# A decoder layer on one core: the bias and the sums of weight tiles in another order on the DMA queues

## The chip, the core and the metric

The kernel runs on one core of one Trainium2 chip. A core has five engines with instruction streams of their own: TensorE (PE in the profile) for matrix products, VectorE (DVE) and ScalarE (ACT) for elementwise work, GpSimd (POOL) and SyncE (SP). The streams wait for each other by semaphores. DMAs are issued by an engine's stream, each of which is worked off in order, and all of them share the core's 16 DMA engines. The metric is the time of one execution on the device in microseconds (us); lower is better.

## The reference

One layer: RMS norm, a pooling mixer with a residual, RMS norm, a gated feed-forward net with a short convolution, and a residual. x is 1024 rows (sequence) by 1024 columns (model), all in float32; the hidden width is 2816.

```python
def pool_mixer(x, w, b, scale):            # windows 2, 4, 8, 16, one for each quarter of the columns
    ...
        groups.append(window_sum / count - xf[..., gi * POOL_GROUP:(gi + 1) * POOL_GROUP])
    d = jnp.stack(groups, axis=2)
    y = jnp.einsum('bsgc,gcd->bsgd', d, w.astype(jnp.float32)).reshape(bsz, seq, D_MODEL) + b
    return (scale * y).astype(x.dtype)

def conv_ffn(x, w_in, conv_w, conv_b, w_out):
    h = causal_depthwise_conv(x @ w_in, conv_w, conv_b)
    val, gate = jnp.split(h, 2, axis=-1)
    return (jax.nn.silu(gate) * val) @ w_out

def reference(x, ...):
    h = rms_norm(x, norm_mix_g[layer])
    x = x + pool_mixer(h, pool_w[j], pool_b[j], pool_scale[j])
    f = conv_ffn(rms_norm(x, norm_ffn_g[layer]), ffn_w_in[layer], ...)
    return x + f
```

## The kernel before

**Stages.** First the mixer, for eight blocks of 128 rows (x0 to x7). For each block j: statistics of x (`stat`, tiles `st_a`), a band matrix scaled by them (`mixer_norm`, `bandr`), the window sums as products of x with that band (`mixer_window`, PSUM tile `psd`; x is the stationary operand, line 212), the mixer's weights (`mixer_out`, `psy`, line 296), the addition of `psy` to x on VectorE (line 304, in place; the result x1 is stored to `x1_dram`, line 305), statistics again (`st_b`), the second normalization (`ffn_norm`, `n2`, line 316), and a transposition on TensorE (`ffn_operand`, `pst`, line 331). The stages of neighbouring blocks overlap.

Then the first product of the feed-forward net, in a Strassen-like form. x1's normalized transpose and each weight tile are cut in quarters, and seven products (P1 to P7, `STEPS`) of sums of quarters replace eight. The operands made from x1 are B11, B21, T1, B22, T2, T3 and T4. Those of weight tile n (22 tiles; `win`, with quarters a11, a12, a21, a22) are A11, A12, A22 and four sums: S3 = a11 + a21, S1 = a21 + a22 (written into a21), S2 = a11 + S1 (into a11), S4 = a12 + S2 (into a12). So S1 may be made only after S3 has read a21, S2 after S1 and after A11 was split, and S4 after S2 and after A12 was split. Each float32 operand is split into a high part (ScalarE, line 95) and a rest (VectorE, line 96), and a product is three matmuls for each of four steps (line 416). The second product of the net (line 779) follows the same pattern, from memory.

**The bias and the sums by DMA.** For blocks 0 to 3 the mixer's bias is two matmuls more (line 301). For blocks 4 to 7 (`BY_DMA`) GpSimd's queue adds it to x: `bias_into` issues a DMA that accumulates `bias_b`, the bias spread over 128 partitions, into x (line 244). It must come after `psd` of that block has read x, and before line 304. `bias_b` itself is loaded from a row in device memory (line 240). The sums S3, S1, S2 and S4 of tiles 0 and 1 are accumulating DMAs of the same queue (line 373; `sums_in` by its argument `step`), and so are S3 and S1 of all later tiles, whose S2 and S4 VectorE makes. S3 begins as a second load of a11 into a small tile of its own (line 379, SyncE's queue). An accumulating DMA of line 373 moves 256 KB, one of line 244 moves 512 KB.

**What sets the order.** A scheduler places each instruction in its engine's stream from the order in which the code issues it; `tc.issue_after(m)` puts what follows behind instruction m in that order, which is an order of streams and adds no semaphore. The loop at line 531 runs over j and issues for each j: the norm of block j, the window of block j - 1 with its bias, the output of block j - 2 and its norm, the transposition of block j - 4, and then at chosen j the loads and sums of weight tiles 0 and 1 (lines 550 to 561) and their first splits (`prep_event(k)`, where k counts in `events`: 0 and 1 are A11 of tiles 0 and 1, 2 and 3 are A12, 4 and 5 are S1, 6 and 7 are S4, 8 is S2 of tile 0). Line 541 issues event 4; lines 572 to 575 issue events 5 to 8. A stream waits at an instruction until its semaphores have come, and all that is behind it in that stream waits too.

Of the kernel before, what the change touches and what calls it, by code (L numbers as in the profile page):

```python
# [14 lines left out]
P = 128  # L15
S = 1024
D = 1024
F = 2816
NS = S // P
# [30 lines left out]
NH = 512  # L50
# [17 lines left out]
def trunk_kernel(ctx: ExitStack, tc: tile.TileContext, x, consts, par, rows, pool_w, w_in, w_out, out):  # L68
    nc = tc.nc
# [98 lines left out]
    marks = {}  # L168
# [66 lines left out]
    bias_row = dram.tile([1, D], F32, tag="bias_row", name="bias_row")  # L235
    biased = {}

    def bias_spread():
        biased["tile"] = work.tile([P, D], F32, tag="ha", name="bias_b", bufs=1)
        nc.gpsimd.dma_start(biased["tile"], bias_row.to_broadcast([P, D]))  # L240

    def bias_into(j):
        if j >= BY_DMA:
# [2 lines left out]
    def pool_bias():  # L246
        marks["bias"] = nc.scalar.activation(bias8[:, 0, :], b8, AF.Copy).ins
        marks["bias_dve"] = nc.vector.tensor_tensor(bias8[:, 1, :], b8, bias8[:, 0, :].bitcast(F32), ALU.subtract).ins
        nc.gpsimd.dma_start(bias_row.rearrange("o (k p) -> (o k) p", p=P), b8)
        for l in range(2):  # L250
            m = nc.sync.dma_start(bias_hl[l : l + 1, :].bitcast(F32), bias8[:, l, :].bitcast(F32)).ins
        with tc.issue_after(m):
            for j in range(3, NS):
                load_x(j)
            marks["loads"] = nc.sync.dma_start(par_sb[:, :GM], par[:, :GM]).ins

    def gain_rows():
# [33 lines left out]
    def mixer_out(j, stats=True):  # L291
        dh = ds.pop(j)
        ps = bank2(f"psy{j}")
        for c in range(NK):
            o = ps[:, c // 2 * GRP : (c // 2 + 1) * GRP]
            m = nc.tensor.matmul(  # L296
                o, dh[:, c, :P], wps[:, c, :], start=c % 4 == 0, stop=j >= BY_DMA and c % 4 == 3, skip_group_check=True
            )
        for h in range(0 if j >= BY_DMA else 2):
            cols = slice(h * NH, (h + 1) * NH)  # L300
            m = nc.tensor.matmul(ps[:, cols], ones, bias_hl[:, cols], start=False, stop=True, skip_group_check=True)
        marks[f"psy{j}"] = m.ins
        x1 = n2s[j] = xs.pop(j)
        marks[j] = nc.vector.tensor_tensor(x1, ps, x1, ALU.add).ins  # L304
        nc.sync.dma_start(x1_dram[j * P : (j + 1) * P, :], x1)
        if stats:
            mixer_out_stats(j)

# [58 lines left out]
    def tmp(name):  # L367
        return work.tile([P, NH], F32, tag="sum", name=name, bufs=3)

    def sums_in(n, step):  # L370

        def more(out, a):
            nc.gpsimd.dma_start(out, a, accum_op=ALU.add)  # L373

        a11, a12, a21, a22 = (raws[n][:, i, k * NH : (k + 1) * NH] for i in range(2) for k in range(2))
        if step == 0:
            s3 = sums[n, "S3"] = tmp(f"S3_{n}")
            with tc.issue_after(marks["loads"]):
                nc.sync.dma_start(s3, w_in[order[n]][:, 0, :NH])
            more(s3, a21)  # L380
        if step == 0 and n > 1 or step == 2:
            more(a21, a22)
        if step == 1:
            sums[n, "S2"] = a11
            more(a11, a21)
            sums[n, "S4"] = a12
            more(a12, a11)

    def prep_in(n, op):
        a11, a12, a21, a22 = (raws[n][:, i, k * NH : (k + 1) * NH] for i in range(2) for k in range(2))  # L390
        if op in ("S1", "S2") and (n, "S3") not in sums:
            s3 = sums[n, "S3"] = tmp(f"S3_{n}")
            add(s3, a11, a21)
            add(a21, a21, a22)
        if op in ("S2", "S4") and (n, "S2") not in sums:
            sums[n, "S2"] = a11
            add(a11, a21, a11)
        if op == "S4" and (n, "S4") not in sums:
            add(a12, a12, a11)
        if op == "S3":  # L400
            src = sums[n, "S3"]
        else:
            src = {"A11": a11, "A12": a12, "S1": a21, "A22": a22, "S2": a11, "S4": a12}[op]
        log = []
        aops[n, op] = split(src, f"{op}s_{n}", log)
        marks[op, n] = log[0]
        if op == "A22" and n + 2 < NF:
            load_in(n + 2)
            sums_in(n + 2, 0)

    def product(bank, a, b, opens):
        m = 0
# [104 lines left out]
        mixer_weights(scale_b, range(1, 2 * NG))  # L517
    with tc.issue_after(marks["psd0"]), tc.issue_after(marks["bias"]):
        gains.append(gain_rows())
    with tc.issue_after(marks["gain_load"]):  # L520
        bias_spread()
    with tc.issue_after(marks["gain"]), tc.issue_after(marks["wps"]):
        stat(2)
    with tc.issue_after(marks["gain_pe"]), tc.issue_after(marks["a2"]), tc.issue_after(marks["wps"]):
# [6 lines left out]
    for j in range(2, NS + 4):  # L531
# [17 lines left out]
            ffn_operand(j - 4)  # L549
        if j in (4, 6):  # L550
            load_in(j // 2 - 2)
            sums_in(j // 2 - 2, 0)
        if j in (5, 6):
            with tc.issue_after(biased[j - 1]):
                sums_in(j - 5, 2)
        if 6 <= j <= 8:
            with tc.issue_after(marks[j - 2]), tc.issue_after(marks[f"b{j - 3}"]):
                for k in {6: (0,), 7: (1, 2), 8: (3,)}[j]:
                    prep_event(k)
        if j in (7, 8):  # L560
            sums_in(j - 7, 1)
        if j in (8, 10, 11):
            event((8, 10, 11).index(j))
        stat(j + 1)
# [6 lines left out]
        nops[b] = nop_tile(nop_b, b)  # L571
    for k in range(4, 4 + LOOK):
        if k != 4:
            with tc.issue_after(marks["T1"][1] if k == 8 else marks[NS - 1]):
                prep_event(k)
    s0, s1 = slice(0, NH), slice(NH, S)
    lo, hi = slice(0, 4), slice(4, 8)
# [284 lines left out]
```

## Time and profile before

| | us |
|---|---|
| median of 3 runs (range) | 671.14 (670.97 to 672.75) |
| the profiled execution | 671.28 |
| its span, first to last instruction | 669.6 |
| TensorE busy | 660.2 (99%) |
| VectorE busy | 567.9 (85%) |
| ScalarE busy | 336.6 (50%) |
| GpSimd busy | 53.6 (8%) |
| mean granted TensorE clock | 0.997 |

Busy time of TensorE is modelled and its matmuls overlap, so a busy TensorE isn't one at its peak; waits and the mean spacing of matmuls say more. In a row of the timeline stand the start, the duration, the engine, the line, the instruction, what it writes and reads, and in brackets the idle time before it and what ended that. Buffer numbers are left out of names: `x` may be any of the eight blocks, which then follows from the order. SPq is SyncE's DMA queue. For an issued DMA the duration is that of the issue; its landing comes later and is given by another view, or by the chain of waits, where a row that begins with DMA lasts from issue to landing.

### The profile page before, as it was taken

The numbers are of one execution on the slowest core, as the hardware profiler recorded it, in microseconds if no ns is written. First come the engines' busy times: TensorE is split into PE (matmuls) and PEld (weight loads), VectorE is DVE, ScalarE is ACT, GpSimd is POOL, SyncE is SP. The second block draws the span as 40 slices with busy tenths as digits, with TensorE's granted clock in tenths as the row PEclk, the third lists the DMA queues.
The fourth block names the chain that finished last, engine by engine and source line by source line (L and its number), as shares of the span: only waits on it lengthen the run. The fifth ranks groups of instructions, "written<-read, shape, count | busy, mean of one in ns | idle before, by whom it ended". The sixth has DMA issues, their size and how long they took to land.

```text
span 669.6 us, 8664 instructions
## 1 busy us (share of the span) xinstructions
PE 660.2 (99%) x3126; PEld 575.1 (86%) x3126; DVE 567.9 (85%) x845; ACT 336.6 (50%) x521; POOL 53.6 (8%) x81
## 2 busy tenths in 40 slices
PE   8998999999999999999999999999999999999997
PEld 6897878888888888888888888888888888888886
DVE  5778999998888888888888888887987988999995
ACT  5786655555445544444544444554554444444441
POOL 5022020110011111111001101100000000000000
PEclk9998999999999999999999999999999999999999
DMA  7999263544544454444444444429999810122231
GB/s 233 360 244 209 85 151 125 159 145 122 142 120 111 132 141 142 143 130 125 138 142 127 111 140 125 114 94 332 342 341 342 290 47 1 62 96 80 63 126 63
DMA packets 42386, 103.73 MB, mean 155 GB/s; under 512 B 4796, under 2 KB 6760, under 8 KB 39528
## 3 DMA queue, kind: packets, MB, share of 16 engines
q1 hardware_dynamic: 34464, 87.43, 37.1%
q0 software_dynamic: 7872, 15.75, 13.4%
q8 instruction: 24, 0.39, 0.3%
q14 instruction: 18, 0.15, 0.1%
q10 hardware_dynamic: 8, 0.00, 0.0%
HBM read 68.55 MB, written 19.93 MB: 132 GB/s over the span
## 4 chain that ended last, share of the span: by engine, by line
PE 90%; DMA 4%; DVE 3%; ACT 1%; issue 1%; SPq 0%; POOL 0%; ACTq 0%; POOLq 0%; DVEq 0%
PE oP L779 29%; PE Y L416 25%; PE X L416 17%; PE Z L416 15%; PE psy L296 2%; DMA S<-win 1%; DMA S<-in_w_in_dram 1%; DMA x<-bias_b 1%; DMA cst<-in_consts_dram 1%; DVE T L351 1%; PE pst L331 1%; PE psd L212 0%; DVE x L304 0%; DVE n2f L588 0%; ACT B L350 0%
## 5 line engine op out<-in xcount | busy, mean ns | idle before, releaser
L779 PE MATMUL oP<-oBP,oAP 128*128 128x512 f32 (+1 forms) x924 | 198.9, 378 | 0.1
L779 PEld LDWEIGHTS oP<-oBP,oAP 128*128 128x128 f32 x924 | 174.0, 189 | 25.0 <-DVE oBP L96 0.5
L416 PE MATMUL X<-B,A11s 128*128 128x512 f32 x264 | 61.5, 380 | 0.0
L416 PE MATMUL Y<-T,S3s 128*128 128x512 f32 x264 | 60.8, 380 | 0.4 <-DVE q L445 0.4
L416 PE MATMUL Y<-T,A22s 128*128 128x512 f32 x264 | 60.9, 380 | 0.0
L416 PE MATMUL Z<-T,S1s 128*128 128x512 f32 x264 | 60.8, 379 | 0.0
L416 PE MATMUL X<-B,A12s 128*128 128x512 f32 x264 | 60.7, 379 | 0.0
L416 PE MATMUL Y<-T,S2s 128*128 128x512 f32 x264 | 60.6, 379 | 0.0
L416 PE MATMUL Z<-B,S4s 128*128 128x512 f32 x264 | 60.5, 379 | 0.0
L416 PEld LDWEIGHTS Y<-T,S3s 128*128 128x128 f32 x264 | 49.7, 189 | 8.2 <-DVE q L445 1.2
L416 PEld LDWEIGHTS Y<-T,A22s 128*128 128x128 f32 x264 | 49.7, 189 | 7.9 <-DVE hb L453 0.6
L416 PEld LDWEIGHTS Z<-T,S1s 128*128 128x128 f32 x264 | 49.8, 189 | 7.5 <-DVE T L351 0.4
L416 PEld LDWEIGHTS Z<-B,S4s 128*128 128x128 f32 x264 | 49.8, 189 | 7.3 <-DVE r L450 0.3
L416 PEld LDWEIGHTS Y<-T,S2s 128*128 128x128 f32 x264 | 49.9, 189 | 7.1
L416 PEld LDWEIGHTS X<-B,A11s 128*128 128x128 f32 x264 | 49.7, 189 | 7.3 <-DVE A11s L96 0.4
L416 PEld LDWEIGHTS X<-B,A12s 128*128 128x128 f32 x264 | 49.8, 189 | 7.0
L95 ACT ACTIVATE oBP<-blk 128x512 fp32r<-128x512 f32 x53 | 33.1, 625 | 44.2 <-PE oP L779 30.6
L474 ACT ACTIVATE gate<-gate 128x1024 f32<-128x1024 f32 x22 | 23.2, 1056 | 49.3 <-DVE gate L465 49.3
L95 ACT ACTIVATE oAP<-blk 128x512 fp32r<-128x512 f32 x55 | 34.1, 620 | 19.6 <-DVE blk L362 17.0
L96 DVE TENSOR_TENSOR oBP<-blk,oBP 128x512 fp32r<-128x512 f32 x53 | 36.5, 688 | 8.6 <-ACT oBP L95 6.6
L96 DVE TENSOR_TENSOR oAP<-blk,oAP 128x512 fp32r<-128x512 f32 x55 | 37.7, 685 | 2.9 <-ACT oAP L95 2.9
L373 POOL DMA_DIRECT2D S<-win x22 | 19.2, 873 | 254.0 <-DMA win<-in_w_in_dram 253.4
(157 smaller groups left out, 965.9 us busy)
## 6 DMA issues: line engine op xcount, KB each, us to landing
win<-in_w_in_dram SPq DMA_DIRECT2D x22, 1024.0 KB, 4.9
g_dram<-val SPq DMA_DIRECT2D x22, 512.0 KB, 2.6
blk<-g_dram SPq DMA_DIRECT2D x33, 256.0 KB, 5.3
blk<-in_w_out_dram SPq DMA_DIRECT2D x31, 256.0 KB, 5.2
win<-win POOLq DMA_DIRECT2D x26, 256.0 KB, 3.7
S<-in_w_in_dram SPq DMA_DIRECT2D x22, 256.0 KB, 3.3
S<-win POOLq DMA_DIRECT2D x22, 256.0 KB, 4.2
A12s<-g_dram SPq DMA_DIRECT2D x22, 256.0 KB, 5.2
```

Of the source, the lines that this page charges most:

```text
L95: nc.scalar.activation(t[:, 0, :], src, AF.Copy)
L96: m = nc.vector.tensor_tensor(t[:, 1, :], src, t[:, 0, :].bitcast(F32), ALU.subtract)
L296: m = nc.tensor.matmul(o, dh[:, c, :P], wps[:, c, :], start=c % 4 == 0, stop=j >= BY_DMA and c % 4 == 3, skip_group_check=True)
L331: nc.tensor.transpose(ps[:, c * P : (c + 1) * P], n2[:, c * P : (c + 1) * P], ident)
L351: return hi, nc.vector.tensor_tensor(l, src, h.bitcast(F32), ALU.subtract).ins
L373: nc.gpsimd.dma_start(out, a, accum_op=ALU.add)
L416: nc.tensor.matmul(bank, a[:, i, ks], woven(b[:, l, k, :]), start=opens and m == 0, stop=m == 11, skip_group_check=not opens)
L474: nc.scalar.activation(gate, gate, AF.Silu)
L779: nc.tensor.matmul(bank, a[:, u, i * P : (i + 1) * P], woven(b[:, v, :])[:, c.start // 2 : c.stop // 2, :], start=opens and first, stop=g ...
```

## The change

`bias_b` is loaded by SyncE's queue, between the loads of x4 and x5. `sums_in` takes the names of the parts that it is to issue, and the loop issues them in another order among the bias additions: S3 of tile 0, bias of block 5, S3 of tile 1 and S1 of tile 0, bias of block 6, S2 of tile 0, bias of block 7, then the rest. The second load of a11 (for S3) of tile 2 and of later ones is issued after the store of x1's last block instead of after the first loads. Events 5 to 8 are issued after the second statistics of block 7 as well. The same DMAs are issued as before, with the same bytes, and the engines do the same arithmetic.

```diff
     def bias_spread():
         biased["tile"] = work.tile([P, D], F32, tag="ha", name="bias_b", bufs=1)
-        nc.gpsimd.dma_start(biased["tile"], bias_row.to_broadcast([P, D]))
+        nc.sync.dma_start(biased["tile"], bias_row.to_broadcast([P, D]))
...
             for j in range(3, NS):
                 load_x(j)
+                if j == 4:
+                    bias_spread()
...
-        nc.sync.dma_start(x1_dram[j * P : (j + 1) * P, :], x1)
+        marks[f"x1_{j}"] = nc.sync.dma_start(x1_dram[j * P : (j + 1) * P, :], x1).ins
...
-    def sums_in(n, step):
+    def sums_in(n, *names):
...
-        if step == 0:
-            s3 = sums[n, "S3"] = tmp(f"S3_{n}")
-            with tc.issue_after(marks["loads"]):
-                nc.sync.dma_start(s3, w_in[order[n]][:, 0, :NH])
-            more(s3, a21)
-        if step == 0 and n > 1 or step == 2:
-            more(a21, a22)
-        if step == 1:
-            sums[n, "S2"] = a11
-            more(a11, a21)
-            sums[n, "S4"] = a12
-            more(a12, a11)
+        for name in names:
+            if name == "load":
+                s3 = sums[n, "S3"] = tmp(f"S3_{n}")
+                with tc.issue_after(marks["loads" if n < 2 else f"x1_{NS - 1}"]):
+                    nc.sync.dma_start(s3, w_in[order[n]][:, 0, :NH])
+            elif name == "S3":
+                more(sums[n, "S3"], a21)
+            elif name == "S1":
+                more(a21, a22)
+            elif name == "S2":
+                sums[n, "S2"] = a11
+                more(a11, a21)
+            else:
+                sums[n, "S4"] = a12
+                more(a12, a11)
...
             load_in(n + 2)
-            sums_in(n + 2, 0)
+            sums_in(n + 2, "load", "S3", "S1")
...
-    with tc.issue_after(marks["gain_load"]):
-        bias_spread()
...
             load_in(j // 2 - 2)
-            sums_in(j // 2 - 2, 0)
-        if j in (5, 6):
-            with tc.issue_after(biased[j - 1]):
-                sums_in(j - 5, 2)
+            sums_in(j // 2 - 2, "load")
+        if j == 4:
+            sums_in(0, "S3")
+        if j == 6:
+            with tc.issue_after(biased[5]):
+                sums_in(1, "S3")
+                sums_in(0, "S1")
...
-        if j in (7, 8):
-            sums_in(j - 7, 1)
+        if j == 7:
+            with tc.issue_after(biased[6]):
+                sums_in(0, "S2")
+        if j == 8:
+            with tc.issue_after(biased[7]):
+                sums_in(1, "S1")
+                sums_in(0, "S4")
+                sums_in(1, "S2", "S4")
...
         if k != 4:
-            with tc.issue_after(marks["T1"][1] if k == 8 else marks[NS - 1]):
+            with tc.issue_after(marks["T1"][1] if k == 8 else marks[NS - 1]), tc.issue_after(marks[f"b{NS - 1}"]):
                 prep_event(k)
```

The streams of the two kernels differ in three places that matter here. First GpSimd's queue from the bias of block 4 on, before the change (a row `win0<-win0` is S1, S2 or S4 of tile 0, in that order; the numbers at the ends of names are buffers):

```order
L244 DMA x4_227<-bias_b_250 128x1024
L373 DMA S3_0_416<-win0_414 128x512
L373 DMA win0_414<-win0_414 128x512
L373 DMA S3_1_544<-win1_542 128x512
L244 DMA x5_229<-bias_b_250 128x1024
L373 DMA win1_542<-win1_542 128x512
L373 DMA win0_414<-win0_414 128x512
L244 DMA x6_231<-bias_b_250 128x1024
L373 DMA win1_542<-win1_542 128x512
L244 DMA x7_233<-bias_b_250 128x1024
L373 DMA win0_414<-win0_414 128x512
L373 DMA win1_542<-win1_542 128x512
```

and with it:

```order
L244 DMA x4_227<-bias_b_229 128x1024
L375 DMA S3_0_416<-win0_414 128x512
L244 DMA x5_231<-bias_b_229 128x1024
L375 DMA S3_1_543<-win1_541 128x512
L375 DMA win0_414<-win0_414 128x512
L244 DMA x6_233<-bias_b_229 128x1024
L375 DMA win0_414<-win0_414 128x512
L244 DMA x7_235<-bias_b_229 128x1024
L375 DMA win1_541<-win1_541 128x512
L375 DMA win0_414<-win0_414 128x512
L375 DMA win1_541<-win1_541 128x512 x2
```

The bias of block 5 has moved ahead of S1 of tile 0 and of S3 of tile 1, and that of block 7 ahead of S1 of tile 1; all three sums of tile 1 (S1, S2, S4) now stand behind the last bias.

Second, SyncE's queue from the load of x4 on, before:

```order
L110 DMA x4_227<-in_x_dram 128x1024
L110 DMA x5_229<-in_x_dram 128x1024
L110 DMA x6_231<-in_x_dram 128x1024
L110 DMA x7_233<-in_x_dram 128x1024
L255 DMA par_sb_124<-in_par_dram 128x176
L305 DMA x1_dram_150<-x0_134 128x1024
L305 DMA x1_dram_150<-x1_138 128x1024
L359 DMA win0_414<-in_w_in_dram 128x2048
L379 DMA S3_0_416<-in_w_in_dram 128x512
L359 DMA win1_542<-in_w_in_dram 128x2048
L305 DMA x1_dram_150<-x2_144 128x1024
L379 DMA S3_1_544<-in_w_in_dram 128x512
```

and with the change:

```order
L110 DMA x4_227<-in_x_dram 128x1024
L240 DMA bias_b_229<-bias_row_149 128x1024
L110 DMA x5_231<-in_x_dram 128x1024
L110 DMA x6_233<-in_x_dram 128x1024
L110 DMA x7_235<-in_x_dram 128x1024
L257 DMA par_sb_124<-in_par_dram 128x176
L307 DMA x1_dram_150<-x0_134 128x1024
L307 DMA x1_dram_150<-x1_138 128x1024
L361 DMA win0_414<-in_w_in_dram 128x2048
L307 DMA x1_dram_150<-x2_144 128x1024
L382 DMA S3_0_416<-in_w_in_dram 128x512
L361 DMA win1_541<-in_w_in_dram 128x2048
```

The load of `bias_b` is new in this queue. The store of x1's block 2 now stands ahead of the S3 load of tile 0 and of tile 1's load; the S3 load of tile 2, which stood right behind the last row shown of before, now comes after the store of block 7.

Third, ScalarE around the end of the mixer, before (`S1s_1` is the split of S1 of tile 1, `st_b7` the second statistics of block 7, `q1` and `ha` are copies of products out of PSUM):

```order
L95 ACTIVATE S1s_0_683<-win0_414 128x512
L95 ACTIVATE S1s_1_793<-win1_542 128x512
L343 ACTIVATE n2f_151<-pst4_649 128x4x2x64
L180 ACTIVATE junk_b6_639,st_b6_640<-x6_231 128x1024
L350 ACTIVATE T1_153<-n2f_151 128x8x64
L181 ACTIVATE st_b6_640<-st_b6_640,eps_t_87 128x1
L439 ACTIVATE q1_0_681<-X0_668 128x512
L95 ACTIVATE S4s_0_796<-win0_414 128x512
L343 ACTIVATE n2f_151<-pst5_707 128x4x2x64
L180 ACTIVATE junk_b7_697,st_b7_698<-x7_233 128x1024
L343 ACTIVATE n2f_151<-pst6_721 128x4x2x64
L181 ACTIVATE st_b7_698<-st_b7_698,eps_t_87 128x1
```

and with the change:

```order
L345 ACTIVATE n2f_151<-pst5_707 128x4x2x64
L180 ACTIVATE junk_b7_697,st_b7_698<-x7_235 128x1024
L352 ACTIVATE T1_153<-n2f_151 128x8x64
L181 ACTIVATE st_b7_698<-st_b7_698,eps_t_87 128x1
L345 ACTIVATE n2f_151<-pst6_721 128x4x2x64
L95 ACTIVATE S1s_1_793<-win1_541 128x512
L95 ACTIVATE S4s_0_796<-win0_414 128x512
L352 ACTIVATE T1_153<-n2f_151 128x8x64
L444 ACTIVATE q1_1_748<-X1_735 128x512
L95 ACTIVATE S4s_1_799<-win1_541 128x512
L95 ACTIVATE S2s_0_802<-win0_414 128x512
L447 ACTIVATE ha0_776<-X0_668 128x512
```

The split of S1 of tile 1 and that of S4 of tile 0 have moved behind `st_b7`, and one half of the T1 operand now stands ahead of them.

## The prediction, made before the changed kernel ran

> **What bounds the kernel now.** I read the page first, for the span and the granted TensorE clock in 40 slices.
>
> ```profile
> span 669.6 us, 8664 instructions
> ...
> PEclk9998999999999999999999999999999999999999
> ```
>
> TensorE is the bound nearly everywhere, at full clock: only the fourth slice (50 to 67 us) falls to 8 tenths. So what can be won lies where TensorE waits or is slow, and for that I read the waits of the first 130 us.
>
> ```profile
> DVE x L304 <- DMA x<-bias_b: 5.8, 2, 4.2
> ...
> PE psy L296 <- DVE x L304: 2.3, 1, 2.3
> ```
>
> VectorE's addition of the mixer's output to x (line 304) waits 5.8 us, in two pieces, for GpSimd's DMA that adds the bias to x; behind the longer piece (4.2) TensorE waits 2.3 us. The chain of waits (start, us, what) shows what comes before and after.
>
> ```profile
> 33.37 8.63 DMA S<-win
> ...
> 43.59 7.64 DMA x<-bias_b
> ...
> 52.60 5.41 PE psy L296 x16
> ...
> 61.47 3.45 PE psy L296 x16
> ```
>
> The bias DMA at 43.59 lands at 51.23, just before the addition. The 16 matmuls of the next `psy` then take 5.41 us, the same 16 later 3.45. The stretches of 1 us give the reason (last three numbers: granted clock, DMA share, GB/s):
>
> ```profile
> 53.00:54.00 1.00, 1.00 (x4) 0.83 (x3) 1.00 (x3) 0.95 (x3) 0.56 (x2) 0.50 1.17 205
> ...
> 56.00:57.00 1.00, 1.00 (x6) 0.83 (x5) 0.95 (x1) 1.00 (x3) 0.07 (x1) 0.81 1.00 279
> ```
>
> The clock is at half from 53 to about 56.4 us. So the place costs TensorE 2.29 us of waiting (the row at 52.60 less the end of the matmuls at 49.69, 50.30) and 5.41 - 3.45 = 1.96 us of slow matmuls: **4.25 us**. No other place of this trace shows such a loss.
>
> **Why the bias is late.** TensorE had released the x tile (block 5) much earlier:
>
> ```profile
> 37.33 0.65 PE L212 MATMUL psd5x<-bandr,x 128*128 128x144 f32 x4
> ...
> 43.54 0.65 PE L212 MATMUL psd6x<-bandr,x 128*128 128x144 f32 x4
> ...
> 44.03 3.62 PE L296 MATMUL psy<-wps,dh 128*128 128x256 f32 x16
> ...
> 49.69 0.61 PE L212 MATMUL psd7x<-bandr,x 128*128 128x128 f32 x4
> ```
>
> The bias for block 5 may go once `psd5` has read x, at 37.98. It went at 43.59. GpSimd's queue (start, us of the issue) shows what stood ahead of it:
>
> ```profile
> 42.51 0.85 POOL L373 DMA_DIRECT2D win<-win  x1 [8.27 <-DVE bandr L189]
> ...
> 43.05 1.19 POOL L373 DMA_DIRECT2D S<-win  x1
> ...
> 43.59 1.53 POOL L244 DMA_DIRECT2D x<-bias_b  x1
> ...
> 49.92 1.55 POOL L244 DMA_DIRECT2D x<-bias_b  x1
> ...
> 53.97 1.21 POOL L244 DMA_DIRECT2D x<-bias_b  x1
> ...
> 60.66 0.86 POOL L373 DMA_DIRECT2D win<-win  x1 [4.59 <-DVE A12s L96]
> ```
>
> The three x rows are blocks 5, 6 and 7. Ahead of block 5 stand S1 of weight tile 0 at 42.51, which could go only when S3 of that tile (33.37 + 8.63 = 42.00) had landed, and S3 of tile 1. VectorE, meanwhile:
>
> ```profile
> 45.83 1.28 DVE L316 SCALAR_TENSOR_TENSOR n<-x,st_b,gain_b 128x1024 f32<-128x1024 f32 x1
> ...
> 51.32 1.23 DVE L304 TENSOR_TENSOR x<-psy,x 128x1024 f32<-128x1024 f32 x1 [4.21 <-DMA x<-bias_b]
> ...
> 58.54 1.23 DVE L304 TENSOR_TENSOR x<-psy,x 128x1024 f32<-128x1024 f32 x1 [1.59 <-DMA x<-bias_b]
> ```
>
> It is idle from 47.11 to 51.32 (4.21) and again 1.59 us for block 6. `psy` of block 5 is done at 44.03 + 3.62 = 47.65, so block 5's addition could have run 3.7 us earlier.
>
> **The change, part by part.**
>
> *Order in GpSimd's queue.* No DMA is added; block 5 goes ahead of S3 and S1. It now has only S3 of tile 0 before it. That waits for its load on SyncE's queue, where the change puts the store of x1 block 2 first:
>
> ```profile
> 24.01 0.47 SPq L359 DMA_DIRECT2D win<-in_w_in_dram  x1
> ...
> 24.53 0.67 SPq L379 DMA_DIRECT2D S<-in_w_in_dram  x1
> ...
> 25.39 0.53 SPq L359 DMA_DIRECT2D win<-in_w_in_dram  x1
> ...
> 29.84 0.33 SPq L305 DMA_DIRECT2D x_dram<-x  x1
> ...
> 30.21 1.25 SPq L379 DMA_DIRECT2D S<-in_w_in_dram  x2
> ```
>
> The load is issued after 29.84 instead of at 24.53, about 5.7 us later, and the second weight tile (25.39) as much. From issue to its use at 33.37 the load took at most 8.84 us before; with the same it would be usable at 39.05, at worst. At best it has only 0.79 MB (the store and itself) to move. Rates come from the DMA view of 30 to 66 us:
>
> ```profile
> q0 software_dynamic: 1721, 4.19, 64.2%
> ...
> q1 hardware_dynamic: 1276, 4.43, 33.7%
> ...
> win<-win POOLq DMA_DIRECT2D x6, 256.0 KB, 5.4
> ```
>
> In these 36 us the accumulating queue took 36 x 0.642 / 4.19 = 5.5 us per MB and SyncE's 36 x 0.337 / 4.43 = 2.7. An accumulate of 256 KB costs the engines 1.45 us, one of 512 KB 2.9; a plain 512 KB costs 1.44, and the weight tile 2.9. The engines are full here (97.9% together), so I make the landings a running sum from 29.84. Until block 5's bias is done there are: store 1.44, S3 load 0.72, tile 1 2.87, its S3 load 0.72, block 4's bias 2.89, S3 of tile 0 1.45, a store 1.44, block 5 2.89, in all 14.4, so 44.3. It is wanted at 47.65. With the whole 7.64 us of its row from 38.5, it lands at 46.2. Even held until 39.05 plus the 0.88 us or so of an issue, it comes at 47.6. So **block 5's wait goes: -2.29 us**, and as TensorE then has no gap, the half clock goes too: **-1.96 us**.
>
> *What is late next.* Without the gap `psy` of block 6 follows `psd7` at 50.30 and ends near 53.7. Block 6's bias may go at 44.19 (after `psd6`); the sum goes on by S3 and S1 (1.45 each), a store and itself to 51.5. So 1.59 us of VectorE waiting goes too, but TensorE is then the later one, and I count nothing for it (if all of it counted, 4.21 + 1.59 = 5.80 would be the most that the change can bring). Block 7's bias goes after 50.30 and the sum gives 57.3; it is wanted at 61.31 + 3.45 - 4.25 = 60.5.
>
> *The parts of tile 1.* They are moved behind block 7, one after the other, as each reads what the last wrote: S1, S2, S4. In the sum S1 is in at 58.7. S2 and S4 follow: at least 2 x 1.45 more (61.6), at most twice the median row of 5.4 and 0.54 for an issue (43.05 to 43.59), which gives 70.6. I take 67.7, two thirds of the way up: the engines are less full by then, but the 5.4 holds more than packets. The last reader is ScalarE's split of S4:
>
> ```profile
> 46.98 0.65 ACT L95 ACTIVATE A11s<-win 128x512 fp32r<-128x512 f32 x1
> ...
> 69.80 0.62 ACT L95 ACTIVATE S4s<-win 128x512 fp32r<-128x512 f32 x1
> ...
> 71.98 0.63 ACT L95 ACTIVATE S2s<-win 128x512 fp32r<-128x512 f32 x1 [1.56 <-DVE n L316]
> ...
> 73.20 0.60 ACT L343 ACTIVATE n2f<-pst 128x512 f32<-128x512 f32 x1
> ```
>
> From that split at 69.80 to the copy of the last transposed block at 73.20 lie 3.40 us, 1.56 of them idle, so 1.84 of work stands in ScalarE's queue behind S4. The copy would start 4.25 earlier, at 68.95; S4 must be there by 67.1. At 67.7 it is 0.6 late. **+0.6 us** (0 to 3.5). What waits for that copy is VectorE's T1, and TensorE's products of it:
>
> ```profile
> 72.09 1.06 PE L331 MATMUL pst<-cst,n 128*128 128x128 f32 x8
> ...
> 75.37 5.60 PE L416 MATMUL Z<-T,S1s 128*128 128x512 f32 x24
> ```
>
> *Three splits later.* Line 574's new condition puts three splits of weight parts behind the statistics of block 7. S1 of tile 1 is used only after 12 matmuls of the row at 75.37, and VectorE gets one T1 subtraction less ahead of the last normalization in exchange. Cost 0; were the cover gone, a split is 0.62 us.
>
> *The bias's spread.* It moves from GpSimd's queue to SyncE's, ahead of the loads of blocks 5 to 7, with the same 512 KB.
>
> ```profile
> L110 SPq DMA_DIRECT2D x<-in_x_dram x1: 430/430/430, 13.7 to 13.7; - x1
> ...
> DMA to landing us min/median/max: 7.6/7.6/7.6
> ...
> 25.03 1.04 ACT L180 ACTIVATE junk_a<-x 128x1024 bf16<-128x1024 f32 x1
> ```
>
> Block 5's load landed at 21.3 and is read first at 25.03. One more transfer ahead costs it 1.44 us by the rate above: 22.7. It costs 0 while those 3.7 us cover it; without cover, 1.4.
>
> *The S3 load of tile 2* (the second of the two issues at 30.21) goes behind the last store. It frees 0.7 us of full engines; it is added to only when tile 2 has come, after the products of tile 0. Cost 0. Tile 1 comes some 6 us later; its first split ran at 46.98, when the sum above has it in by 36, so 0.
>
> **Sum.** -2.29 - 1.96 + 0.6 = -3.65. The profiled execution took 671.28 us (span 669.6 and 1.7 around it), 0.14 over the median of the runs: 667.6, or **667.5 us** beside the median of 671.14.
>
> **The rivals.**
>
> *B, the slow clock has another cause.* [...] If the half clock came from something else, it would come again, and the change would bring 3.65 - 1.96 = 1.7: 669.5.
>
> *C, the wait moves to block 6.* Its bias stands behind S1 of tile 0, which waits for S3's accumulate. If the S3 load needs its 8.84 again (39.05) and the accumulate its 8.63 (47.7), block 6 goes at 48.2 and lands 7.64 later, at 55.9, 2.2 after `psy`. VectorE is that much late; it had about 1 us of reserve before TensorE needs the last normalization, so 1.2 of the gain go: 668.8. Against it: the engines' sum has both in 4 us earlier.
>
> *D, slower: the serial parts of tile 1.* S1, S2 and S4 of tile 1 now all lie behind block 7. With block 7 landing at 50.9 + 7.64 = 58.5, S1 at 60.0, one of the other two as slow as the 8.63 row, one at 5.4, and two issues, S4 is in at 75.1. ScalarE then stands still with the last copies behind it, and the start of T1's products is 75.1 - 67.1 = 8.0 late against 4.25 won: +3.75, 674.9. It decides from a landing of 71.4 on (67.1 + 4.25). For it: before, only S2 and S4 came behind block 6. Against it: the bytes hardly change, and the sum has S1 in at 58.7, with only the last two stores beside S2 and S4.
>
> **Chances.** Forecast 0.62, B 0.11, C 0.14, D 0.13. Within 0.3% (2.0 us, about what runs of this kernel can tell from no change) lie B, a third of C and little of the forecast; so faster 0.70, same 0.17, slower 0.13. The range begins at 671.14 - 5.80, 665.4, and reaches to the forecast with its S4 term at 3.5 (670.4), over B and C: 665.4 to 670.6. It leaves out D.
>
> **What would show it.** Right: line 304 no longer waits for the bias, `psy` of block 6 starts near 50.3 and takes 3.45, the granted clock is 1.00 in every slice after the start, and the products of T1 start near 71.7. The order is shown wrong if block 5's bias is issued later than 40, the S4 term if ScalarE waits over 1 us for S4 of tile 1. A half clock without a wait before it would prove B; a wait of line 304 for block 6, C; an S4 landing after 71.4, D. A difference that arises after 130 us would be none of these.

## The result, and the profile after

The changed kernel takes **667.88 us** (667.48 to 669.01, 6 runs) against 671.16 of the kernel before (670.97 to 672.75, 6 runs of the same comparison): a ratio of 0.9949, 95% interval 0.9936 to 0.9962. The prediction was 667.5 in a range of 665.4 to 670.6, with 0.70 on faster. The profiled execution took 667.48 us. Of all executions compared below one, of number 3, ran in a slower state (692.11 us at a mean granted clock of 0.949), and it isn't counted. First the page of the changed kernel, which answers to the two lines shown of before:

```profile
span 665.8 us, 8664 instructions
...
PEclk9999999999999999999999999999999999999999
```

The fourth slice of the clock, 8 tenths before, is 9 or more, like all others. The waits of the first 130 us (what waited, for what: us in total, times, longest):

```profile
ACT S4s L95 <- DMA win<-win: 1.8, 1, 1.8
...
DVE x L306 <- DMA x<-bias_b: 1.0, 1, 1.0
```

Line 306 (304 before) waited 5.8 us for the bias; 1.0 is left. ScalarE's wait for S4 of tile 1 is new at this place. VectorE's additions of blocks 5, 6 and 7:

```profile
47.45 1.23 DVE L306 TENSOR_TENSOR x<-psy,x 128x1024 f32<-128x1024 f32 x1 [0.25 <-PE psy L298]
...
54.13 1.23 DVE L306 TENSOR_TENSOR x<-psy,x 128x1024 f32<-128x1024 f32 x1 [1.04 <-DMA x<-bias_b]
...
60.42 1.23 DVE L306 TENSOR_TENSOR x<-psy,x 128x1024 f32<-128x1024 f32 x1
```

Block 5 waits for nothing but the matmuls. Block 6 has the 1.04. GpSimd's queue shows why (S3 of tile 0, bias 5, S1 of tile 0, bias 6, bias 7, S4 of tile 1):

```profile
36.99 0.87 POOL L375 DMA_DIRECT2D S<-win  x1 [4.49 <-DMA S<-in_w_in_dram]
...
38.23 0.85 POOL L244 DMA_DIRECT2D x<-bias_b  x1 [0.37 <-ACT st_b L181]
...
45.15 0.85 POOL L375 DMA_DIRECT2D win<-win  x1 [1.37 <-DVE psd6x L284]
...
45.69 1.19 POOL L244 DMA_DIRECT2D x<-bias_b  x1
...
52.07 1.20 POOL L244 DMA_DIRECT2D x<-bias_b  x1
...
64.55 0.86 POOL L375 DMA_DIRECT2D win<-win  x1 [3.60 <-DVE st_b L184]
```

Block 5's bias goes at 38.23, not 43.59, about half a microsecond after `psd5` has read x (37.68). The view of that one DMA gives its landing:

```profile
L244 POOL DMA_DIRECT2D x<-bias_b x1: 851/851/851, 38.2 to 38.2; - x1
...
DMA to landing us min/median/max: 9.1/9.1/9.1
```

38.23 + 9.1 = 47.3, when the addition was wanted at 47.45. So it was in time by about 0.1 us, and not by the 3 that the prediction's running sum gave (44.3). Block 6's had to follow S1 of tile 0 at 45.15, which waited for S3's accumulate, issued at 36.99 and in 7.6 later, at 44.6. On TensorE:

```profile
49.40 0.61 PE L212 MATMUL psd7x<-bandr,x 128*128 128x128 f32 x4
...
49.84 3.62 PE L298 MATMUL psy<-wps,dh 128*128 128x256 f32 x16
...
53.30 1.04 PE L333 MATMUL pst<-cst,n 128*128 128x128 f32 x8
...
67.58 1.06 PE L333 MATMUL pst<-cst,n 128*128 128x128 f32 x8 [0.26 <-DVE n L318]
...
71.54 0.46 PE L421 MATMUL Z<-T,S1s 128*128 128x512 f32 x1 [0.31 <-ACT T L352]
...
72.24 5.23 PE L421 MATMUL Z<-T,S1s 128*128 128x512 f32 x23 [0.24 <-DVE T L353]
...
86.73 2.86 PE L421 MATMUL Y<-T,S3s 128*128 128x512 f32 x12 [0.41 <-DVE q L450]
```

`psy` of block 6 follows `psd7` without a wait and its 16 matmuls are over by 53.30 or so, where the next row begins, 3.46 after their start. The products of T1 start at 71.54 instead of 75.37, but with two short pauses (0.31 and 0.24). ScalarE has their cause, the split of S4 of tile 1 with the copy behind it:

```profile
67.96 0.64 ACT L95 ACTIVATE S4s<-win 128x512 fp32r<-128x512 f32 x1 [1.79 <-DMA win<-win]
...
69.49 0.59 ACT L345 ACTIVATE n2f<-pst 128x512 f32<-128x512 f32 x1
```

The start of an execution shifts by some tenths of a microsecond from run to run, here by 49.69 - 49.40 = 0.29. I therefore measure from the row of `psd7x` to the first product with S3 of tile 0, which the kernel before had at

```profile
90.44 2.86 PE L416 MATMUL Y<-T,S3s 128*128 128x512 f32 x12 [0.41 <-DVE q L445]
```

that is 90.44 - 49.69 = 40.75 before and 86.73 - 49.40 = 37.33 after: **3.42 us** gained between these two points. A second profile of each kernel gives 40.78 (number 8) and 37.30 (number 11).

### The profile page after: what moved, and what is told of

Read it like the earlier page. It is cut to its first block, busy times and chain, and to the rows that moved or that the text cites. A ratio compares the mean times of both kernels' runs of the same rounds, so it can differ in the third digit from the quotient of the medians.

```text
span 665.8 us, 8664 instructions
## 1 busy us (share of the span) xinstructions
PE 658.3 (99%) x3126; PEld 573.9 (86%) x3126; DVE 567.8 (85%) x845; ACT 336.6 (51%) x521; POOL 53.0 (8%) x80
## 4 chain that ended last, share of the span: by engine, by line
PE 95%; DVE 2%; ACT 1%; issue 1%; DMA 1%; POOL 0%; ACTq 0%; POOLq 0%
PE oP L791 29%; PE Y L421 25%; PE X L421 16%; PE Z L421 16%; PE psy L298 4%; PE psd L212 2%; PE pst L333 1%; DVE T L353 1%; DMA win<-win 1%; PE idle_ps L152 0%; DVE n2f L600 0%; PE ps_scale L224 0%; ACT B L352 0%; PE psy L303 0%; DVE oBP L96 0%
## 5 line engine op out<-in xcount | busy, mean ns | idle before, releaser
L469 DVE SCALAR_TENSOR_TENSOR val<-ha,par_sb,val 128x1023 f32<-128x1023 f32 x22 | 28.2, 1282 | 13.2 <-ACT val L468 13.2
```

Source lines behind the costliest of these rows:

```text
L469: nc.vector.scalar_tensor_tensor(t[:, 1:], src[:, : S - 1], w[1], t[:, 1:], op0=ALU.mult, op1=ALU.add)
```

## The experiments

The theory: the gain is the wait for block 5's bias and what followed from it, and the order of GpSimd's queue brings it; the spread, the load and the splits bring nothing by themselves. Rivals: one of the other edits carries it; the half clock is a separate loss, or none at all; what is left (the S4 wait, block 6's wait) is or is not on the path to the end.

### 1. The order undone, everything else kept

```diff
-        if j == 4:
-            sums_in(0, "S3")
-        if j == 6: ... sums_in(1, "S3"); sums_in(0, "S1")
...
+            sums_in(j // 2 - 2, "load", "S3")
+        if j in (5, 6):
+            with tc.issue_after(biased[j - 1]):
+                sums_in(j - 5, "S1")
...
-        if j == 7: ... sums_in(0, "S2")
-        if j == 8: ... sums_in(1, "S1"); sums_in(0, "S4"); sums_in(1, "S2", "S4")
+        if j in (7, 8):
+            sums_in(j - 7, "S2", "S4")
```

> The changed kernel with GpSimd's queue in the order of before; the bias's spread on SyncE's queue, the later splits and the later load stay. My theory (the order carries the gain): S3 of tile 0 still gets its load only near 36.9, its accumulate lands near 45, so S1 goes at 45 and block 5's bias at about 46, landing near 53.5; line 306 waits about 6 us for it, TensorE 4.5, the clock goes to half for some 3.4 us, and the time is 671 to 674. Rival (the other edits carry the gain, or part of it): 667.5 to 669.5, with a wait of line 306 under 2 us.

Measured: 673.38 us (673.10 to 673.89) against 670.93, ratio 1.0036, interval 1.0022 to 1.0049: slower than the kernel before. VectorE's additions of blocks 5 and 6:

```profile
50.95 1.23 DVE L306 TENSOR_TENSOR x<-psy,x 128x1024 f32<-128x1024 f32 x1 [3.66 <-DMA x<-bias_b]
...
60.75 1.23 DVE L306 TENSOR_TENSOR x<-psy,x 128x1024 f32<-128x1024 f32 x1 [4.17 <-DMA x<-bias_b]
```

Both wait, 3.66 and 4.17, because the S3 load is later than before and all else stands behind it: S3's accumulate goes at 36.69, not 33.37, and block 5's bias at 45.29, not 43.59. So there is no gain without the order, and the other edits, without it, make it worse. TensorE's pauses:

```profile
52.23 3.72 PE L298 MATMUL psy<-wps,dh 128*128 128x256 f32 x16 [1.74 <-DVE x L306]
...
66.55 1.06 PE L333 MATMUL pst<-cst,n 128*128 128x128 f32 x8 [2.81 <-DVE n L318]
...
73.97 1.06 PE L333 MATMUL pst<-cst,n 128*128 128x128 f32 x8 [1.17 <-DVE n L318]
```

They sum to 5.72, and in this execution the clock stayed at 1.00 throughout, against the expectation of a half clock. In two of the four executions the mean clock was 0.997, so some stretch there had a lower clock.

### 2. The three splits as before, everything else kept

```diff
-            with tc.issue_after(...), tc.issue_after(marks[f"b{NS - 1}"]):
+            with tc.issue_after(...):
```

> The changed kernel with the three splits issued as before. In the changed kernel S1 of tile 1 lands near 59.6; with this edit ScalarE's split of it stands again right behind the split of S1 of tile 0, near 53.6. Theory 1 (the later splits belong to the order and pay for it): ScalarE waits about 6 us there, the copies and the statistics of block 6 behind it are as late, TensorE waits some 4 us for the transposes and loses clock again: 672 to 675. Rival, as the prediction had it (the place of the splits costs and brings nothing): 667.5 to 668.3.

Measured: 672.21 us (671.79 to 673.91, 10 runs) against 670.93, ratio 1.0019, interval 1.0010 to 1.0029. ScalarE's split of S1 of tile 1, then TensorE's transposes:

```profile
60.19 0.63 ACT L95 ACTIVATE S1s<-win 128x512 fp32r<-128x512 f32 x1 [6.28 <-DMA win<-win]
```

```profile
65.58 1.94 PE L333 MATMUL pst<-cst,n 128*128 128x128 f32 x8 [3.96 <-DVE n L318]
```

and the clock, the third number from the end, in one of the stretches of 2 us behind that pause:

```profile
66.00:68.00 2.00, 2.00 (x10) 1.91 (x9) 2.00 (x4) 0.80 (x1) 0.00 (x0) 0.50 0.76 130
```

The clock was at half for 6.8 us, from 64.8 to 71.6, in this execution, the longest of the ten; the mean clock was 0.997 or less in all ten. The time is 1.28 us above the kernel before of the same comparison, where the changed kernel was 3.28 below its own: with the new order the three later splits are worth about 4.6 us, what the half clock cost included. The prediction had priced their place at nothing. And the new order without the later splits, the spread and the load in place, is slower than the kernel before: the gain needs both.

### 3. The split of S4 of tile 1 behind the last copy

```diff
+        marks[f"n2f{j}"] = <the copy of the transposed block>.ins
...
-            with tc.issue_after(marks["T1"][1] if k == 8 else marks[NS - 1]), ...
+            with tc.issue_after(marks["T1"][1] if k == 8 else marks[f"n2f{NS - 1}"] if k == 7 else marks[NS - 1]), ...
```

> The changed kernel with the split of S4 of tile 1 issued behind the copy of the last transposed block (one more condition). Theory: its wait of 1.79 us no longer holds up that copy, which starts near 68.5 instead of 69.49; T1 is done 0.8 to 1 us earlier, TensorE's pauses of 0.31 and 0.24 at 71.5 go, and the time falls by 0.5 to 0.9, to about 667.2. Rival: VectorE is the bound from there on and what it has to do in the next 40 us is unchanged, so the start of T1's products moves but the end does not: within 0.2 us of the changed kernel.

Measured: 667.50 us (667.27 to 667.71, 4 runs) against 670.93, ratio 0.9947, interval 0.9933 to 0.9961. That is the changed kernel's ratio (0.9949), so neither answer is shown: a gain of 0.5 would lie inside the interval.

### 4. The bias of block 5 added twice

```diff
-            biased[j] = nc.gpsimd.dma_start(xs[j], biased["tile"], accum_op=ALU.add).ins
+            for _ in range(2 if j == 5 else 1):
+                biased[j] = nc.gpsimd.dma_start(xs[j], biased["tile"], accum_op=ALU.add).ins
```

> The changed kernel with the bias added to block 5 twice, by two DMAs one after the other (so block 5's output is off by one bias): it puts the wait back without touching the order. Theory (the half clock follows the wait): the second lands near 52, line 306 waits about 4.5 us, TensorE 2 to 3 us, then runs at half clock for some 3.4 us, and the time is 671 to 672.5. Rival B (the half clock had another cause): the wait is there, the clock stays at 1.00, and the time is 669.5 to 670.5.

Measured: 674.06 us (672.67 to 675.69) against 670.93, ratio 1.0046, interval 1.0030 to 1.0062: more than expected. The wait for block 5 came back (4.73 us on line 307), and TensorE paused twice:

```profile
53.10 3.72 PE L299 MATMUL psy<-wps,dh 128*128 128x256 f32 x16 [2.81 <-DVE x L307]
...
79.11 1.49 PE L422 MATMUL Z<-T,S1s 128*128 128x512 f32 x2 [4.52 <-ACT T L353]
```

The second pause wasn't expected. GpSimd's queue stood still for 7.71 us before the second of the two additions; block 6's bias then went 3.0 us later than in the changed kernel (48.68 against 45.69), and S4 of tile 1 7.7 later (72.22 against 64.55). The clock behind each of the two:

```profile
52.00:54.00 2.00, 0.90 (x4) 0.82 (x5) 2.00 (x3) 0.92 (x1) 0.00 (x0) 1.00 1.13 191
...
80.00:82.00 2.00, 2.00 (x5) 1.63 (x6) 2.00 (x3) 1.98 (x3) 0.00 (x0) 0.50 0.01 4
```

After 2.81 us it stayed full; after 4.52 it was halved. So the theory that the half clock follows this wait fails here: the wait came back at the same place, somewhat longer, and cost no clock.

### 5. The spread on GpSimd's queue, everything else kept

```diff
-        nc.sync.dma_start(biased["tile"], bias_row.to_broadcast([P, D]))
+        nc.gpsimd.dma_start(biased["tile"], bias_row.to_broadcast([P, D]))
```

(issued after `gain_load`, as before)

> The changed kernel with the bias's spread on GpSimd's queue as before; order, later splits and later load stay. The S3 load of tile 0 then stands ahead of the store of x1's block 2 again, goes near 24.2 and is in near 33, so S3's accumulate goes near 33 instead of 36.99 and S1 of tile 0 no longer holds block 6's bias back. Theory (the spread's queue is worth nothing by itself, as the prediction had it, and the later S3 load costs a little): block 6's bias goes near 44.6 and line 306's wait of 1.04 us for it goes; the time is 667.2 to 667.9, no more than the changed kernel. Rival (the spread on SyncE's queue is part of the gain): line 306 waits for block 5 again and the time is 668.6 or more.

Measured: 667.85 us (667.56 to 668.41) against 670.86, ratio 0.9956, interval 0.9943 to 0.9968. Block 6's wait is gone and the time is that of the changed kernel, so no gain shows from its going. By itself this doesn't prove that the wait cost nothing, for ScalarE's wait for S4 of tile 1 grew from 1.79 to 2.14. The second load of a11 for tile 2, the accumulate of S4, and the split that waits for it:

```profile
62.51 12.06 SPq L380 DMA_DIRECT2D S<-in_w_in_dram  x2
```

```profile
63.29 0.86 POOL L373 DMA_DIRECT2D win<-win  x1 [4.34 <-DVE n2f L362]
```

```profile
68.77 0.63 ACT L95 ACTIVATE S4s<-win 128x512 fp32r<-128x512 f32 x1 [2.14 <-DMA win<-win]
```

The accumulate goes 0.8 us behind that load and is in at about 68.7, 5.4 after its issue; in the changed kernel it took 3.4.

### 6. The order and the later splits alone

The kernel before with these two edits; the spread and the load as before.

```diff
-                with tc.issue_after(marks["loads" if n < 2 else f"x1_{NS - 1}"]):
+                with tc.issue_after(marks["loads"]):
```

(against the changed kernel, with the diff of number 5)

> The kernel of before with the order of the sums and the later splits alone (spread and load as before). Theory: that is the whole gain, 667.3 to 668.2. Rival: the S3 load of tile 2, which then runs near 31 again, takes 0.7 us of full DMA engines ahead of block 5's bias, which came only just in time in the changed kernel (landed near 47.3, wanted at 47.45): line 306 waits up to 0.7 us for block 5, 668.3 to 669.

Measured: 667.27 us (666.68 to 667.43) against 670.86, ratio 0.9946, interval 0.9931 to 0.9961. No wait of line 304 for any bias, no wait for S4. It is 0.58 under number 5, from which it differs by the load alone, and no run of the one reaches the other's. From `psd7x` to the product with S3 it takes 36.53 in the trace, against 37.68 in number 5.

### 7. Numbers 3 and 5 together

> The changed kernel with the spread on GpSimd's queue and the split of S4 of tile 1 behind the copy of the last transposed block: both waits that the changed kernel has left (1.04 us of line 306 for block 6, 1.79 us of ScalarE for S4) should be gone. If the waits that are left are on the path to the end: 666.6 to 667.2. If VectorE's work from 70 us on sets the end whatever comes before: within 0.3 us of the changed kernel (667.6 to 668.0).

Measured: 667.58 us (667.28 to 667.85) against 670.86, ratio 0.9950, interval 0.9938 to 0.9963. Both waits are gone from its trace, and it is 0.27 under number 5 and not under number 6. Between the two points it takes 37.04, between 37.68 (5) and 36.53 (6), which would mean that to split S4 later repairs part of what the later load does; by times the 0.27 isn't told from nothing. With both waits gone the ratio is still the changed kernel's.

### 8. The kernel before, profiled again

> The kernel of before, profiled once more. If the half clock belongs to its wait of 2.3 us, the profile shows it again near 53 us, with psy of block 6 at about 5.4 us, and 671. [...]

Measured: 671.33 us. The half clock was there again, from 52.6 to 56, at the end of a wait of 2.41 us, and `psy` took 5.32. But it doesn't come in every execution of this kernel. In the three comparisons that hold numbers 1 to 12 it ran 45 times: 24 times with a mean granted clock of 0.996 or 0.997, 21 times at 1.000. The 24 took 0.5 to 0.7 us longer on average (in the largest set 671.43, 13 runs, against 670.95, 8 runs). What goes with the half clock is thus worth some 0.5 us and not 1.96; whether the clock does it, or a wait that was shorter in the others, the next two bear on.

### 9. The kernel before, with TensorE kept busy in its wait

```diff
+        if j == 6:
+            busy = ps_x.tile([P, NH], F32, tag="X", name="busy")
+            for _ in range(10):
+                nc.tensor.matmul(busy, ones, bias_hl[:, :NH], start=True, stop=True)
```

> The kernel of before with ten matmuls of ones by the bias (results unused) between psd7 and psy of block 6, some 2.2 us that fill TensorE's wait; the waits of VectorE stay. The clock should stay at 1.00 and psy of block 6 take 3.45. Theory 1 (as the prediction summed it: the half clock's 1.96 us lie on the path): 669.0 to 669.6. Theory 2 (VectorE's second wait, for block 6's bias until 58.54, and the work behind it end at 64.80, only 0.16 before the addition of block 7 that waited for TensorE; so the slow matmuls were covered): 670.6 to 671.2, with the addition of block 7 at most 0.2 us earlier.

Measured: 671.39 us (670.25 to 671.75, 11 runs) against 671.27 (21 runs), ratio 0.9998, interval 0.9990 to 1.0007. The clock and TensorE in its trace:

```profile
53.00:54.00 1.00, 1.00 (x7) 0.87 (x6) 1.00 (x3) 0.95 (x4) 0.84 (x2) 1.00 1.17 215
```

```profile
49.94 2.53 PE L296 MATMUL busy<-bias_hl,ones 128*128 128x512 f32 x10
...
52.32 3.72 PE L300 MATMUL psy<-wps,dh 128*128 128x256 f32 x16
...
71.98 1.06 PE L335 MATMUL pst<-cst,n 128*128 128x128 f32 x8 [1.55 <-DVE n L320]
...
75.25 4.96 PE L420 MATMUL Z<-T,S1s 128*128 128x512 f32 x21
```

The clock is full (0.999 or more in all 11 executions), `psy` takes 3.72 in its row, and next to nothing is won: what the faster matmuls gain is waited for at 71.98, and from `psd7x` to the first product of T1 it takes 75.25 - 49.57 = 25.68, as in the kernel before (75.37 - 49.69). Against the 13 half-clock executions of the kernel before alone the mean is 0.28 lower (671.15 to 671.43), with ranges that overlap. VectorE still had its second wait, and ScalarE waited longer for S4 of tile 0 (3.29, 1.59 before), which stands ahead of the statistics of block 7:

```profile
58.17 1.22 DVE L308 TENSOR_TENSOR x<-psy,x 128x1024 f32<-128x1024 f32 x1 [1.49 <-DMA x<-bias_b]
```

```profile
65.21 0.64 ACT L95 ACTIVATE S4s<-win 128x512 fp32r<-128x512 f32 x1 [3.29 <-DMA win<-win]
```

So in the kernel before nearly all of the half clock's 1.96 us was covered by VectorE, as theory 2 said, and here also by ScalarE, which theory 2 didn't name.

### 10. The later splits alone

```diff
-            with ..., tc.issue_after(marks["T1"][1] if k == 8 else marks[NS - 1]):
+            with ..., tc.issue_after(marks["T1"][1] if k == 8 else marks[NS - 1]), tc.issue_after(marks[f"b{NS - 1}"]):
```

> The kernel of before with the three later splits alone. In the order of before their operands are in early enough for either place, and the wait for block 5 sets the pace: 670.6 to 671.4 (no change). Rival (the earlier place costs something in the old order too): 669 to 670.

Measured: 671.17 us (670.57 to 671.77) against 671.27, ratio 0.9997, interval 0.9988 to 1.0006: nothing, as expected. In its trace the wait was shorter,

```profile
50.13 0.61 PE L212 MATMUL psd7x<-bandr,x 128*128 128x128 f32 x4
...
52.41 3.72 PE L296 MATMUL psy<-wps,dh 128*128 128x256 f32 x16 [1.67 <-DVE x L304]
...
89.72 2.86 PE L416 MATMUL Y<-T,S3s 128*128 128x512 f32 x12 [0.41 <-DVE q L445]
```

and the clock stayed full after it (0.999 on average over the execution). This execution is the fastest of the ten, 670.57, and takes 89.72 - 50.13 = 39.59 between the two points, 1.16 less than the kernel before; 0.62 of that is the shorter wait. Six of the ten had a mean clock of 0.997 and took 671.35 on average, the other four 670.80, the same 0.5 as in number 8. So the later splits are worth nothing here, but an execution without the half clock does gain a little, with a shorter wait beside it.

### 11 and 12. The changed kernel, and order with splits alone, in one comparison

> The changed kernel once more, beside the next run on the same chip: 667.5 to 668.0, with ScalarE's wait of 1.8 us for S4 of tile 1 and line 306's wait of 1.0 for block 6.

> The order and the later splits alone, once more. Theory (the spread and the later load each bring a wait of their own and no gain): 0.5 to 0.8 us under the changed kernel of the same call, near 667.2, with neither of its two waits. Rival (the first comparison was chance): within 0.3 us of it.

Measured: the changed kernel 668.11 us (667.74 to 668.20), ratio 0.9950 (0.9938 to 0.9963); order and splits alone **666.97 us** (666.82 to 667.60), ratio 0.9938 (0.9925 to 0.9952), against 671.27. The two intervals overlap, but the runs of the two kernels, on one chip in one comparison, don't: 1.14 us lie between the medians. (Number 6 and the first runs of the changed kernel, each against the kernel before of its own comparison, are only 0.3 apart.) Of the kernel with order and splits alone, TensorE, S4 of tile 1 in GpSimd's queue, and its split:

```profile
49.47 0.61 PE L212 MATMUL psd7x<-bandr,x 128*128 128x128 f32 x4
...
67.65 1.06 PE L331 MATMUL pst<-cst,n 128*128 128x128 f32 x8 [0.26 <-DVE n L316]
...
71.14 5.60 PE L419 MATMUL Z<-T,S1s 128*128 128x512 f32 x24
...
86.00 2.86 PE L419 MATMUL Y<-T,S3s 128*128 128x512 f32 x12 [0.41 <-DVE q L448]
```

```profile
62.09 0.86 POOL L373 DMA_DIRECT2D win<-win  x1 [3.20 <-DVE x L304]
```

```profile
66.12 0.64 ACT L95 ACTIVATE S4s<-win 128x512 fp32r<-128x512 f32 x1
```

S4 goes at 62.09, not 64.55, its split waits for nothing, and the pauses at the start of T1's products are gone. From `psd7x` to the product with S3 it takes 86.00 - 49.47 = 36.53: 4.22 less than before, against 3.42 for the whole change. So the spread and the later load together lose 0.80 of the 4.22 that order and splits bring; the other pair of profiles, numbers 11 and 6, gives 37.30 - 36.53 = 0.77. This version beats both kernels. The load alone on top of the changed kernel wasn't undone; that it can make the S4 wait rests on numbers 5 and 6, which differ by it.

## Why the prediction was right, step by step

**The bound and the cause** held: the order of GpSimd's queue had made block 5's bias late (number 1), and with the new order the wait is gone. The size of the first two terms together, 4.25, is what order and splits alone brought between the two points, 4.22. In the changed kernel it is there in full at block 7's addition, which comes 60.42 - 49.40 = 11.02 after `psd7x` instead of 64.96 - 49.69 = 15.27: 4.25 earlier.

**The split into 2.29 and 1.96 doesn't hold as two losses.** The step "as TensorE then has no gap, the half clock goes too: -1.96" took the half clock for a loss of its own on the path. With the half clock taken away and VectorE's waits kept (9), next to nothing was won, and executions that didn't have it were some 0.5 faster, with the wait possibly shorter too (8, 10). The kernel before had two chains that ended at block 7's addition almost together: TensorE's, with 2.29 of waiting and 1.96 of slow matmuls, and VectorE's, with its waits of 4.21 and 1.59 for the two biases. VectorE's row of that addition in the kernel before shows how near:

```profile
64.96 1.22 DVE L304 TENSOR_TENSOR x<-psy,x 128x1024 f32<-128x1024 f32 x1 [0.16 <-PE psy L296]
```

It waited 0.16 us for TensorE; with TensorE 1.96 us earlier and all else the same it would have gained just that 0.16. The prediction counted the 1.59 as nothing and the 1.96 in full; each was the cover of the other, and the sum was right because the change removed both. The sizes were a little off as well: the 3.45 leaves out what overlaps the matmuls before (that `psy` has 3.62 in its row of the timeline, 5.41 the other), and the 2.29 begins only at the end of `psd7x`. From `psd7x` to `psy` of block 6 it took 2.91 before and 0.44 after, 2.47 less; from the start of that `psy` to the next row, in the kernel before

```profile
57.84 1.04 PE L331 MATMUL pst<-cst,n 128*128 128x128 f32 x8
```

it took 5.24 before and 3.46 after, 1.78 less. The two errors cancel in the 4.25.

**The S4 term**, +0.6 with a landing at 67.7, measured 4.22 - 3.42 = 0.80 with a landing at 64.55 + 3.4 = 67.9. So the size was nearly right. But ScalarE waited 1.79 for that sum, over the 1 us that the prediction itself had named as the sign that this term is wrong; ScalarE came to it early enough to lose only half of the wait. And the cause was named wrongly in part: it is not the place of tile 1's sums behind block 7 alone (numbers 6 and 12 have the same and no wait), but with it the spread and the later load. With the spread S4 goes 15.15 us after `psd7x` (64.55 - 49.40), without it 13.42 (5) and, without the later load too, 12.62 (12); with the later load behind block 7 and the spread as before, its landing took 5.4 instead of 3.9 (12). What each of the two does in the changed kernel isn't separated.

**"Cost 0" for the load and for the splits failed, in opposite directions.** Without the spread, the later load of tile 2 brings the S4 wait by itself (5 against 6, 0.58 us in the time). The splits' cover was priced at 0.62 "were the cover gone"; in the new order it is about 4.6 (number 2), since ScalarE works in order and 6.28 us of waiting at one split hold up the copies and the statistics behind it (they start at 60.73 and 61.21 there, at 54.37 and 55.38 in the changed kernel). The place of the splits was priced in the old order, where it is worth nothing (10), and not in the new one.

**The spread** cost block 5's load what was said. It was predicted at 22.7; its row:

```profile
L110 SPq DMA_DIRECT2D x<-in_x_dram x1: 430/430/430, 13.9 to 13.9; - x1
...
DMA to landing us min/median/max: 8.9/8.9/8.9
```

13.9 + 8.9 = 22.8, and the ScalarE statistics weren't late (24.74, without a wait). It is also what puts the S3 load of tile 0 behind a store (in number 5 that load is ahead of it again). The prediction had counted that under the order, but had block 6's bias, which stands behind S1, in at 51.5; it came at 54.0 (45.69 + 8.3). That is rival C's mechanism, and it happened, but no gain shows where its 1.04 us are gone (5 and 7).

**The running sum of DMA work** came out early for every bias: 44.3 against 47.3, 51.5 against 54.0, 57.3 against 58.6. It laid the transfers end to end from the time the first was issued, while the accumulates waited in GpSimd's queue for each other (S1 of tile 0, issued at 45.15, for S3, in at 44.6). The bounds from the rows were safer (46.2 and 47.6 for the first). The sum promised a margin of 3 us for block 5 where there was 0.1; that it sufficed was in part luck.

**Rival D**, the serial sums of tile 1, has its mechanism in number 4 (S4 late, a pause of 4.52), but not in the changed kernel. **Rival B** in the form it had is refuted: the half clock left with the wait, and in all 11 executions of the changed kernel the mean clock was 0.999 or more. In another form it was nearer than the forecast: the removal of the half clock was worth little by itself.

## What to carry to other kernels

Before a stall's cost is booked, follow the other engine's chain to the point where both meet: the slow matmuls behind a wait were nearly free here, because VectorE was there only 0.16 us sooner. In a queue that works in order, an edit that moves a transfer must be priced together with the edits that move its readers, in the new order and not in the old one: the same three splits were worth nothing in the old and about 4.6 us in the new. And edits that "cost nothing" are worth a run without them: two of the four here together lost a fifth of the gain.

## What the runs showed of the hardware

The granted clock didn't follow the length of TensorE's wait. It fell to half after waits of 2.29 (kernel before) and 2.41 (number 8), and after 3.96 and 4.52 (numbers 2 and 4); it stayed full after 1.67 (10), 1.74 and 2.81 (1) and 2.81 (4). Nor was it the same in every execution of one kernel: 24 of 45 executions of the kernel before had a mean clock of 0.997 or less, 21 had 1.000. In the profiled executions it was half for 3.4 us each time (kernel before, 53.0 to 56.4; number 8, 52.6 to 56.0; number 4, 79.0 to 82.4), in number 2 for 6.8, twice as long. A wait of 2.81 left the clock full and one of 2.29 halved it; what decides between the two, these runs don't show.
